# Joint blocks all begun early, and early gate blocks of the last feed-forward as fills of the second sequence

## The chip, the cores and the metric

The kernel runs on one core of a Trainium2 chip. The time is that of the device, in microseconds, from one launch of the whole program; the runs given are separate executions of the same program. One further execution was recorded by the hardware profiler, and all rows below come from it. Engines are named as in the profile: PE (TensorE) multiplies and transposes into PSUM, DVE (VectorE), ACT (ScalarE) and POOL (GpSimd) work elementwise, SP issues most of the DMAs. The engines run on their own, each through its instructions in a fixed order, and wait for one another by semaphores.

## The reference

One layer of an encoder, in float32, over two sequences of 512 tokens ("prompt" and "sample") of width 1024:

- a SwiGLU feed-forward, `x + 0.5 * (silu(n @ w_gate) * (n @ w_up)) @ w_down` with `n = rms_norm(x)` and 2816 hidden columns;
- a mixing block on `h = rms_norm(x)` and `proj = h @ w_in`: grouped-query attention (8 query heads of 64, 2 key heads, RMS norm of queries and keys, rotary angles, softmax over all 512 tokens), and beside it a bidirectional mLSTM with 4 heads of 128, whose gates are 16 columns of the projection; both are projected up, gated by `sigmoid` of further columns, added, and go through `w_out` onto `x`;
- a second SwiGLU feed-forward, and a final RMS norm.

Both sequences use the same weights and do not depend on each other.

## The kernel before

Every product is done in three matmuls on values split into a high part and a remainder (`split`, `put`, `w_pair`: a copy on ACT that rounds, and a subtraction on another engine), each 128 x 128 by 512 columns.

**Seven products for eight.** In the feed-forwards and in the "joint" projections, the two sequences (and two halves of the inner dimension, and two weight columns) form a 2 x 2 block product, done in seven products (Strassen's scheme in Winograd's form): `B11, B21, B22, T1..T4`. The right sides `xc[...]` are made from both sequences by `right_sums` (line 281). Of a block's seven products, two (`B11`, `B21`) need the first sequence only. So a block can be *begun* (`Up.begin`, line 441, and `Joint.begin`, line 755): 24 matmuls into PSUM, evicted through a ring `k` of two tiles and stored to DRAM (`kept`). The *rest* (`gu_rest`, line 350, and `Joint.block`) has five products, 60 matmuls; a block that was not begun has all 84. While the second sequence's sides are still being made, 10 blocks of each feed-forward (of 22) and 10 of the joint (of 14) are begun; `ORDER` and `JORDER` then alternate begun and whole blocks. The left sides are made per block from the raw weights by `gu_left_a`, `gu_left_b` and `gu_left_c`, and the results of a pair of blocks are turned into the right sides of the down product by `Sides`.

**Program order and queues.** The program is written as a sequence of Python calls; a tile framework then orders each engine's instructions by priority (the place in the program, shifted by `shifted(n)`) and by when operands are there, and adds the waits. So what stands early in the program tends to run early, and work that is listed together is interleaved.

**The stages.** First feed-forward (to about 650 us): begin, rest, `ffn_down`. Joint (to about 940): 14 blocks that give both sequences' merge gates, output gates, and mLSTM queries and keys, parked in `jbuf`; blocks 10 to 13, queries and keys, are stored split. Then `mix(s, ...)` for `s = 0` and `s = 1`, a generator that the program advances with `next`: per-token projections (`tok_proj`), *rotations* (gates, key and query norm and rotary, with transposes on PE), attention (`scores`, `attend`, eight heads), memory heads (`mem_head`, `mem_out`, four), merge (`merge_mem`, eight units), output product (`out_unit`, eight units of 24 matmuls). A list `queue` holds units with which PE is filled between heads: `fill(fills[h])` after each of the eight attention heads and four memory heads takes as many units as the table `FILLS` says, `fill(99)` takes the rest. The first sequence's fills are projections of the second one's queries and values (eight units of 48 narrower matmuls), the second one's are six of the first sequence's output units. `prep2` normalises the first sequence's rows for the last feed-forward. Last come that feed-forward and its down product with the final norm.

The order of the second half of the mix, before:

```
    next(m1)                  # second sequence: rotations
    next(m0)                  # first: merge
    outs0, acc0_ = next(m0)
    go(*outs0[:OUT])          # OUT = 2 output units
    queue.extend(outs0[OUT:])
    next(m1)                  # second: attention, memory heads, with fills
```

## Time and profile before

| | |
|---|---|
| median of 3 runs | 2169.08 us (2168.52 to 2169.25) |
| the profiled execution | 2165.41 us |
| its span, first to last instruction | 2163.6 us |
| mean granted clock of PE over the span | 0.978 |
| PE busy | 2070.3 us, 96% |
| DVE busy | 1677.2 us, 78% |
| ACT busy | 944.9 us, 44% |
| POOL busy | 93.1 us, 4% |

A row of stages gives, for a stretch of the span, each engine's busy time and its number of instructions, the clock that the throttle granted to PE as a share of full speed, and the share of the DMA engines. A row of groups gives line, engine, operation, output and inputs, shape and count, then busy time and mean duration in nanoseconds, then the engine's idle time just before them and what ended it. A row of the timeline gives start and duration in us. Rows of the DMA view end with the median us from issue to landing. POOL's spans are rough, and the line numbers are those of the kernel before.

### The profile page before, as it was taken

Reading aid. Unit: us, or ns where it says so; the run is one execution under the profiler, and the core shown is the slowest. Engines: PE = TensorE matmul, PEld = TensorE weight load, DVE = VectorE, ACT = ScalarE, POOL = GpSimd, SP = SyncE. Lnnn points to the kernel's source line nnn. Section 1 sums busy time; section 2 is a strip of 40 time slices with the busy share of each in tenths; the row PEclk is TensorE's granted clock in tenths of the full one; section 3 lists DMA queues with packets and bytes.
Section 4 is the critical chain, followed back from the end, with each engine's and each line's share of the span. In section 5 each row is a group of like instructions: output and inputs, shape, how many; then the busy total and the mean of one; then the engine's idle time right before and its main releaser. Section 6 shows DMA issues by size and latency. Waiting matters only on the chain.

```text
span 2163.6 us, 27752 instructions
## 1 busy us (share of the span) xinstructions
PE 2070.3 (96%) x9502; PEld 1691.9 (78%) x9502; DVE 1677.2 (78%) x3043; ACT 944.9 (44%) x1744; POOL 93.1 (4%) x106
## 2 busy tenths in 40 slices
PE   8999999999998999999998596899999999999998
PEld 6888888888877788888786474678888888888887
DVE  7888887877898877655878787674888888786697
ACT  6544444432234433354666355442544444443222
POOL 0000000000012000000001110102000000000000
PEclk9999999999999999999999698999999999999999
DMA  8655654798757555586256341578855565499753
GB/s 275 192 193 172 219 185 146 256 360 316 251 190 226 162 170 173 145 296 227 88 186 218 108 165 59 195 251 297 267 161 178 193 198 170 159 338 352 270 211 113
DMA packets 332557, 450.70 MB, mean 208 GB/s; under 512 B 21488, under 2 KB 198720, under 8 KB 331392
## 3 DMA queue, kind: packets, MB, share of 16 engines
q1 hardware_dynamic: 330544, 443.46, 60.9%
q0 software_dynamic: 1872, 5.46, 0.8%
q8 instruction: 75, 1.23, 0.2%
q14 instruction: 66, 0.54, 0.1%
HBM read 288.25 MB, written 160.60 MB: 207 GB/s over the span
## 4 chain that ended last, share of the span: by engine, by line
PE 84%; DVE 8%; DMA 3%; ACT 3%; issue 1%; POOL 0%; SPq 0%; DVEq 0%; ACTq 0%; POOLq 0%
PE pss L333 22%; PE pst L333 14%; PE mm L333 11%; PE mm L589 8%; PE mm L915 5%; PE pst L589 4%; PE pss L589 4%; PE pso L589 2%; PE mm L867 2%; PE mm L898 2%; PE pss L1206 1%; PE pst L1225 1%; PE pso L1233 1%; PE pso L1356 1%; PE pss L915 1%
## 5 line engine op out<-in xcount | busy, mean ns | idle before, releaser
L333 PE MATMUL mm<-xc,w 128*128 128x512 f32 x1392 | 334.8, 392 | 6.9 <-DVE f L752 2.5
L333 PE MATMUL pss<-xc,w 128*128 128x512 f32 x1392 | 337.3, 391 | 0.2 <-DVE t L364 0.2
L333 PE MATMUL pst<-xc,w 128*128 128x512 f32 x1392 | 334.7, 389 | 0.0
L333 PEld LDWEIGHTS mm<-xc,w 128*128 128x128 f32 x1392 | 261.0, 189 | 65.4 <-DVE w L292 4.3
L333 PEld LDWEIGHTS pss<-xc,w 128*128 128x128 f32 x1392 | 259.8, 188 | 60.8 <-DVE t L364 6.8
L333 PEld LDWEIGHTS pst<-xc,w 128*128 128x128 f32 x1392 | 261.3, 188 | 54.3
L291 ACT ACTIVATE w<-t 128x512 fp32r<-128x512 f32 x232 | 140.8, 627 | 183.4 <-issue 55.2
L292 DVE TENSOR_TENSOR w<-t,w 128x512 fp32r<-128x512 f32 x232 | 155.8, 690 | 69.1 <-ACT w L291 66.6
L589 PE MATMUL mm<-rt,w 128*128 128x512 f32 (+1 forms) x819 | 188.6, 384 | 0.0
L589 PEld LDWEIGHTS mm<-rt,w 128*128 128x128 f32 x819 | 151.2, 188 | 29.8
L333 PE MATMUL pss<-xc,f 128*128 128x512 f32 x696 | 167.3, 389 | 0.1
L333 PEld LDWEIGHTS pss<-xc,f 128*128 128x128 f32 x696 | 130.6, 188 | 27.6 <-DVE t L797 0.5
L657 ACT ACTIVATE w<-wr 128x512 fp32r<-128x512 f32 x72 | 45.1, 632 | 138.2 <-PE pso L589 71.1
L657 ACT ACTIVATE w<-t 128x512 fp32r<-128x512 f32 x82 | 51.8, 632 | 108.1 <-PE pst L589 63.1
L292 DVE TENSOR_TENSOR w<-wr,w 128x1024 fp32r<-128x1024 f32 x58 | 72.7, 1257 | 28.4 <-ACT w L291 28.4
L589 PE MATMUL pss<-rt,w 128*128 128x512 f32 x396 | 93.8, 389 | 0.4 <-issue 0.4
L589 PE MATMUL pst<-rt,w 128*128 128x512 f32 x396 | 93.6, 389 | 0.0
L915 PE MATMUL mm<-mh,w 128*128 128x512 f32 x256 | 85.2, 406 | 1.9 <-ACT w L239 1.3
L589 PEld LDWEIGHTS pss<-rt,w 128*128 128x128 f32 x396 | 74.2, 188 | 16.2 <-ACT w L657 0.8
L589 PEld LDWEIGHTS pst<-rt,w 128*128 128x128 f32 x396 | 74.3, 188 | 15.4
L291 ACT ACTIVATE w<-wr 128x1024 fp32r<-128x1024 f32 x58 | 61.2, 1056 | 52.2 <-PE pst L333 21.6
L658 DVE TENSOR_TENSOR t<-pst,t 128x512 fp32r<-128x512 f32 x96 | 64.8, 688 | 22.6 <-ACT t L657 19.2
(356 smaller groups left out, 3537.2 us busy)
## 6 DMA issues: line engine op xcount, KB each, us to landing
rt<-rbuf SPq DMA_DIRECT2D x154, 512.0 KB, 5.5
wr<-in_ffn_w_gate_dram SPq DMA_DIRECT2D x62, 512.0 KB, 5.4
rbuf<-tab SPq DMA_DIRECT2D x102, 256.0 KB, 4.0
wpark<-w SPq DMA_DIRECT2D x48, 512.0 KB, 3.6
wr<-in_w_in_dram SPq DMA_DIRECT2D x45, 512.0 KB, 4.4
wr<-in_ffn_w_up_dram SPq DMA_DIRECT2D x44, 512.0 KB, 4.6
rbuf<-f SPq DMA_DIRECT2D x72, 256.0 KB, 3.8
rbuf<-R SPq DMA_DIRECT2D x68, 256.0 KB, 4.0
```

The source lines that it names most:

```text
L291: pin(nc.scalar.activation(t[:, 0], src, AF.Copy))
L292: pin(V_.tensor_tensor(t[:, 1], src, f(t[:, 0]), op=ALU.subtract))
L333: nc.tensor.matmul(p, a[:, k, :], xt[:, b, k, :], start=(first and k == 0 and i == 0), stop=(k == HK_ - 1 and i == 2), skip_group_check=True)
L589: nc.tensor.matmul(p, u[:, a, d * P:(d + 1) * P], r[:, b, ts], start=(first and q == 0 and k == 0), stop=(q == len(us) - 1 and k == 2), sk ...
L657: nc.scalar.activation(hi, src, AF.Copy)
L658: (eng or V_).tensor_tensor(lo, src, f(hi), op=ALU.subtract)
L867: nc.tensor.matmul(p[b][:, :N], a[:, bs], w_[:, kl, :], start=(k == 0 and i == 0), stop=(k == KD - 1 and i == 2))
L898: nc.tensor.matmul(p[b // 2][:, (b % 2) * HW:(b % 2 + 1) * HW], a[:, bs], w_[:, kl, :], start=(k == 0 and i == 0 and b % 2 == 0), stop=(k ...
L915: nc.tensor.matmul(p, a[:, k, :], b, start=(k == 0 and i == 0), stop=(k == n - 1 and i == 2))
L1206: nc.tensor.matmul(p, qT[:, h, b * P:(b + 1) * P], kv[:, hk * 2 + j, :], start=(j == 0), stop=(j == 1))
L1225: nc.tensor.transpose(p[:, b * P:(b + 1) * P], Ps[b][:, kb * P:(kb + 1) * P], ident)
L1233: nc.tensor.matmul(po, Vst[:, kv_, hk, :], w, start=(kv_ == 0 and i == 0), stop=(kv_ == 3 and i == 1))
```

## The change

- **Joint:** all 14 blocks are begun (`JORDER` has no whole block left); begun blocks 10 to 13 take the tile for their high part from the ring `k`. In the joint's preparation the remainders of `B22` and `T3` are made on POOL.
- **Mix, first sequence:** the rotations stand in the program ahead of the value projection and of the second sequence's key projection. The second sequence's values are parked in DRAM (`vpark`) by `rows_ahead` and split in its memory heads by `parked_values`.
- **Mix, order:** the first sequence's merge comes before the second's rotations; then all eight output units are issued, then statistics and `prep2`, all ahead of the second's attention.
- **Fills of the second sequence:** eight gate blocks of the last feed-forward are begun there (`Up.early`, `EARLY = 8`), each with a weight split, 24 matmuls, a copy and a Silu on ACT, and two stores. The last feed-forward begins ten more in its own preparation, so 18 of its 22 blocks are begun; its order (`order_of`) spreads the four whole ones among 16 begun. The first feed-forward keeps its order.
- **Engines:** the softmax scaling (`tensor_scalar` in `scores`) goes from DVE to POOL in both sequences; the mask add of `mem_rows` goes to POOL in the second too; query and key tiles of the second come from the buffers `w8` instead of `wr`; the last of each sequence's sums of squares (`sq_add` in `done1`) goes from POOL to DVE.

```diff
@@ -278,14 +278,14 @@
...
-    def right_sums(xc, k, x0l, x0u, x1l, x1u):
+    def right_sums(xc, k, x0l, x0u, x1l, x1u, eng=None):
...
         for i, t in ((T1, x0l), (T2_, x1u), (T3, x1l), (T4, x0u)):
-            put(xc[i], k, t)
+            put(xc[i], k, t, eng if i == T3 else None)
@@ -417,19 +417,33 @@
...
     LATER, SOONER = 100,-100
-    AHEAD = 10
+    AHEAD, EARLY = 10, 8
...
     LAST = 2
-    ORDER = [j for p in zip(range(AHEAD - LAST), range(AHEAD, NF)) for j in p]
-    ORDER += list(range(2 * AHEAD - LAST, NF)) + list(range(AHEAD - LAST, AHEAD))
+    def order_of(ahead):
+        begun, whole = list(range(ahead - LAST)), list(range(ahead, NF))
+        out = []
+        while begun or whole:
+            if begun and (not whole or len(begun) * (NF - ahead) >= len(whole) * (ahead - LAST)):
+                out.append(begun.pop(0))
+            else:
+                out.append(whole.pop(0))
+        return out + list(range(ahead - LAST, ahead))
+    ORDERS = [[j for p in zip(range(AHEAD - LAST), range(AHEAD, NF)) for j in p], order_of(AHEAD + EARLY)]
+    ORDERS[0] += list(range(2 * AHEAD - LAST, NF)) + list(range(AHEAD - LAST, AHEAD))
...
-        def __init__(self, xc, wg, wu, rb):
-            self.xc, self.rb = xc, rb
+        def __init__(self, xc, wg, wu, rb, order):
+            self.xc, self.rb, self.order = xc, rb, order
             self.v = [w.rearrange("(k p) c -> p k c", p=P) for w in (wg, wu)]
             self.kept, self.open = {}, None
+        def make_rings(self):
             self.ring = Rings(s=["t2"] * 3, wd=["f2"] * 2, v=["t2"] * 3, h=["t2"] * 5, o=["f2"] * 2 + ["R"] * 2)
@@ -458,8 +472,19 @@
...
+        def early(self, j):
+            def comp(W):
+                self.kept[j] = kept[j]
+                t, u = T2(F32, "f2"), T2(F32, "f2")
+                X = gu_first_a(W, self.xc, t)
+                nc.sync.dma_start(kept[j][0], t)
+                gu_first_b(X, W, self.xc, u)
+                nc.sync.dma_start(kept[j][1], u)
+            return (lambda: self.left(j)), comp
         def rest(self, raw, at=None, hook=None):
-            ring = self.ring
+            ring, ORDER = self.ring, self.order
@@ -502,7 +527,7 @@
...
-    def ffn_down(wd, rb, ring, tail, xres, done, at_step, hook, halves=None):
+    def ffn_down(wd, rb, order_, ring, tail, xres, done, at_step, hook, halves=None):
         n = n_steps
@@ -526,7 +551,7 @@
...
             t = free.pop(0)
-            fb = ORDER[2 * fp + i]
+            fb = order_[2 * fp + i]
             for c in range(2):
@@ -708,9 +733,8 @@
...
     JP += [(768 + h * P, 1280 + h * P) for h in range(4)]
-    NJ, RAW, JAHEAD, JLAST = 14, 10, 10, 4
-    JORDER = [j for p in zip(range(JAHEAD - JLAST), range(JAHEAD, NJ)) for j in p]
-    JORDER += [j for j in range(NJ) if j not in JORDER]
+    NJ, RAW = 14, 10
+    JORDER = [0, 1, 10, 2, 3, 11, 4, 5, 12, 6, 7, 13, 8, 9]
     jbuf = [[[dpool.tile([P, 2, S] if j >= RAW else [P, S], F32, name=f"jbuf{s}_{j}_{u}") for u in range(2)]
@@ -728,10 +752,10 @@
...
-        def out(self, s, j, u, t):
+        def out(self, s, j, u, t, kind="h"):
             to = jbuf[s][j][u]
             if j >= RAW:
-                hi = self.ring("h")
+                hi = self.ring(kind)
                 split(t, hi.bitcast(F32R), t.bitcast(F32R))
@@ -746,11 +770,11 @@
...
-        def first_b(self, X, W, j, t):
+        def first_b(self, X, W, j, t, kind="h"):
             product(X, W[B21], self.xc[B21], False)
...
                 V_.tensor_tensor(t, X, R[0], op=ALU.mult)
-            self.out(0, j, 0, t)
+            self.out(0, j, 0, t, kind)
@@ -764,7 +788,7 @@
...
                 j, X, W = self.open
-                self.first_b(X, W, j, self.ring("k"))
+                self.first_b(X, W, j, self.ring("k"), "k")
             self.open = None
@@ -954,28 +978,29 @@
...
-    def tok_queries_ahead(s, src, half):
+    vpark = dpool.tile([P, 4, S], F32, name="vpark")
+    def rows_ahead(park, s, src, col, half):
         def done(p):
...
                     nc.scalar.activation(t[:, u * HW:(u + 1) * HW], p[b], AF.Copy, scale=r[s][:, b:b + 1])
-                nc.sync.dma_start(qpark[:, 2 * i:2 * i + 2, half * HW:(half + 1) * HW],
+                nc.sync.dma_start(park[:, 2 * i:2 * i + 2, half * HW:(half + 1) * HW],
                                   t.rearrange("p (u c) -> p u c", u=2))
-        return tok_half(src, 0, half, done)
-    def tok_values_ahead(s, src, half):
-        def done(p):
-            if half == 0:
-                value_tile(s)
-            for b in range(4):
-                values_done(s, p[b], b, slice(half * HW, (half + 1) * HW))
-        return tok_half(src, 1792, half, done)
-    FILLS = ((0, 1, 1, 1, 1, 1, 0, 1, 2, 0, 0, 0), (0, 1, 0, 1, 0, 1, 0, 0, 1, 1, 1, 0))
-    def mix(s, src=None, after=None, fills=None):
+        return tok_half(src, col, half, done)
+    def parked_values(s):
+        vm = value_tile(s)
+        for b in range(4):
+            t = T2()
+            nc.sync.dma_start(t, vpark[:, b])
+            split(t, vm[:, 0, b, :], vm[:, 1, b, :])
+    FILLS = ((0, 1, 1, 1, 1, 1, 1, 0, 0, 0, 0, 0), (0, 0, 1, 1, 1, 1, 1, 0, 1, 1, 0, 0))
+    def mix(s, src, fills):
@@ -1126,14 +1151,10 @@
...
         def load_qk(h):
-            if s == 0:
-                t = wpool.tile([P, 4, S], F32R, tag="w8", bufs=4, name=nm("qk"))
-                halves = t[:, 0:2], t[:, 2:4]
-            else:
-                halves = [wpool.tile([P, 2, S], F32R, tag="wr", bufs=4, name=nm("qk")) for _ in range(2)]
-            for u, t in enumerate(halves):
-                nc.sync.dma_start(f(t), jbuf[s][RAW + h][u])
-            qks[h] = [t[:, i] for t in halves for i in range(2)]
+            t = wpool.tile([P, 4, S], F32R, tag="w8", bufs=4, name=nm("qk"))
+            for u in range(2):
+                nc.sync.dma_start(f(t[:, 2 * u:2 * u + 2]), jbuf[s][RAW + h][u])
+            qks[h] = [t[:, i] for i in range(4)]
@@ -1156,8 +1177,7 @@
...
             go(*tok_proj(src, QC, 2, q_done))
-            go(*tok_values(0, src))
-            yield None
+            flush()
         else:
@@ -1174,7 +1194,7 @@
...
             em3 = em.rearrange("p (b s) -> p b s", b=4)
-            (G_, V_)[s].tensor_tensor(em3, eb3, tabs[3][:, d].unsqueeze(1).to_broadcast([P, 4, P]), op=ALU.add)
+            G_.tensor_tensor(em3, eb3, tabs[3][:, d].unsqueeze(1).to_broadcast([P, 4, P]), op=ALU.add)
             return eb3, em3
@@ -1210,7 +1230,7 @@
...
                 V_.reciprocal(c[:, 2:3], c[:, 1:2])
-                V_.tensor_scalar(e, e, c[:, 2:3], None, op0=ALU.mult)
+                G_.tensor_scalar(e, e, c[:, 2:3], None, op0=ALU.mult)
                 Ps.append(e)
@@ -1287,8 +1307,6 @@
...
                 split(mg[:, d, :], mh[:, d, :], ml[:, d, :], G_ if d < 6 and s == 0 else V_)
-                if after:
-                    after(d)
             return up_unit(1, d, mem, done, (PS, PT)[d % 2])
@@ -1366,6 +1384,8 @@
...
         ups = [merge_att(d) for d in range(KD)]
+        if s:
+            parked_values(s)
         load_qk(0)
@@ -1411,10 +1431,12 @@
...
     xc = [None] * 7
-    up = Up(xc, I["ffn1_w_gate"][0], I["ffn1_w_up"][0], rbuf[0])
+    up = Up(xc, I["ffn1_w_gate"][0], I["ffn1_w_up"][0], rbuf[0], ORDERS[0])
+    up.make_rings()
     xins = [I[n][0] for n in ("x_prompt", "x_sample")]
...
-    kept = [[dpool.tile([P, S], F32, name=f"kept{j}_{i}") for i in range(2)] for j in range(AHEAD)]
+    kept = [[dpool.tile([P, S], F32, name=f"kept{j}_{i}") for i in range(2)]
+            for j in range(AHEAD + EARLY)]
@@ -1509,7 +1531,7 @@
...
         nc.sync.dma_start(xbuf[s][:, d, :], xs[s][:, d, :])
-        accs[s] = sq_add(xs[s][:, d, :], accs[s], "R")
+        accs[s] = sq_add(xs[s][:, d, :], accs[s], "R", eng=V_ if d == (KD - 1, DH - 1)[s] else None)
         if s == 0 and d == KD - 1:
@@ -1529,7 +1551,7 @@
...
-    ffn_down(I["ffn1_w_down"][0], rbuf[0], up.ring, tail, xbuf, done1, 7, mix_consts)
+    ffn_down(I["ffn1_w_down"][0], rbuf[0], up.order, up.ring, tail, xbuf, done1, 7, mix_consts)
@@ -1547,27 +1569,27 @@
...
             normed(t, gm, R[s_], kk)
-        for j in ((3,), (4, 5), (6, 7), (8, 9))[k]:
+        for j in ((3, 4), (5, 6, 7), (8, 9, 10), (11, 12, 13))[k]:
             jt.begin(j, jt.left(j))
-        put(xc[B22], k, x1u)
-        right_sums(xc, k, x0l, x0u, x1l, x1u)
+        put(xc[B22], k, x1u, G_)
+        right_sums(xc, k, x0l, x0u, x1l, x1u, G_)
     jt.begun()
...
     src1 = lambda k: (nhl[1][0][:, k, :], nhl[1][1][:, k, :])
-    m0 = mix(0, src0, None, FILLS[0])
+    m0 = mix(0, src0, FILLS[0])
     next(m0)
+    go(*tok_values(0, src0))
     for d in range(KD):
...
     flush()
-    next(m0)
     for hf in range(2):
-        queue.extend(tok_queries_ahead(1, src1, hf))
+        queue.extend(rows_ahead(qpark, 1, src1, 0, hf))
     for hf in range(2):
-        queue.extend(tok_values_ahead(1, src1, hf))
+        queue.extend(rows_ahead(vpark, 1, src1, 1792, hf))
     next(m0)
@@ -1587,15 +1609,19 @@
...
     OUT = 2
-    m1 = mix(1, None, prep2, FILLS[1])
+    m1 = mix(1, None, FILLS[1])
+    next(m0)
     next(m1)
-    next(m0)
     outs0, acc0_ = next(m0)
-    go(*outs0[:OUT])
-    queue.extend(outs0[OUT:])
-    next(m1)
+    go(*outs0)
+    flush()
     acc2[0] = acc0_[0]
     stats2(0)
+    for d in range(KD):
+        prep2(d)
+    up = Up(xc, I["ffn2_w_gate"][0], I["ffn2_w_up"][0], rbuf[1], ORDERS[1])
+    queue.extend(up.early(j) for j in range(EARLY))
+    next(m1)
     next(m1)
@@ -1603,14 +1629,15 @@
...
-    up = Up(xc, I["ffn2_w_gate"][0], I["ffn2_w_up"][0], rbuf[1])
+    up.make_rings()
     raw0 = up.fetch(0)
-    W = [gu_left_a(raw0[0])]
-    up.begin(0, W[0])
+    j0 = EARLY
+    W = [up.left(j0)]
+    up.begin(j0, W[0])
     stats2(1)
-    W += [up.left(j) for j in (1, 2)]
-    up.begin(1, W[1])
-    up.begin(2, W[2])
+    W += [up.left(j0 + j) for j in (1, 2)]
+    up.begin(j0 + 1, W[1])
+    up.begin(j0 + 2, W[2])
     for i in (T2_, T1, T3, B22, T4):
@@ -1621,7 +1648,7 @@
...
         for j in ((3,), (4, 5), (6, 7), (8, 9))[k]:
-            up.begin(j, up.left(j))
+            up.begin(j0 + j, up.left(j0 + j))
         put(xc[B22], k, x1u)
@@ -1706,7 +1733,7 @@
...
-    ffn_down(I["ffn2_w_down"][0], rbuf[1], up.ring, tail, x2buf, done2, n_steps - 7, load_fn, halves=True)
+    ffn_down(I["ffn2_w_down"][0], rbuf[1], up.order, up.ring, tail, x2buf, done2, n_steps - 7, load_fn, halves=True)
...
 def host_consts():

```

## The prediction

> **What bounds the kernel now.** I read the page first, for the shares and the chain, then the time by stages, then the groups of the stages that lose time. The page:
>
> ```profile
> span 2163.6 us, 27752 instructions
> ...
> PE 2070.3 (96%) x9502; PEld 1691.9 (78%) x9502; DVE 1677.2 (78%) x3043; ACT 944.9 (44%) x1744; POOL 93.1 (4%) x106
> ...
> PE 84%; DVE 8%; DMA 3%; ACT 3%; issue 1%; POOL 0%; SPq 0%; DVEq 0%; ACTq 0%; POOLq 0%
> ```
>
> TensorE (PE) bounds the kernel: 96% busy and 84% of the chain. The order of the built instructions shows that the change keeps every product and transpose, so only time that PE now loses can be won. Where it is lost, by stages (columns: width, then busy time and count of each engine, granted clock, DMA share, GB/s):
>
> ```profile
> core 0: us, PE busy (x) PEld busy (x) DVE busy (x) ACT busy (x) POOL busy (x), PEclk, DMA share, GB/s
> 640.00:740.00 100.00, 90.61 (x391) 71.96 (x391) 87.42 (x147) 44.18 (x66) 15.24 (x10) 0.98 0.62 193
> 1010.00:1110.00 100.00, 92.56 (x594) 78.57 (x594) 83.40 (x197) 69.48 (x163) 4.26 (x12) 0.98 0.37 118
> 1110.00:1190.00 80.00, 73.34 (x386) 59.23 (x384) 63.26 (x181) 48.42 (x115) 10.33 (x6) 0.96 0.65 219
> 1190.00:1254.00 64.00, 42.05 (x172) 33.60 (x171) 51.80 (x129) 24.28 (x43) 11.33 (x6) 0.71 0.40 135
> 1254.00:1335.00 81.00, 68.23 (x316) 48.84 (x314) 62.54 (x131) 43.59 (x99) 6.12 (x7) 0.95 0.24 86
> 1335.00:1450.00 115.00, 98.19 (x424) 72.58 (x425) 77.00 (x232) 57.75 (x142) 6.10 (x7) 0.90 0.68 224
> 1450.00:1510.00 60.00, 59.38 (x257) 48.32 (x257) 34.15 (x57) 17.40 (x26) 11.23 (x12) 0.98 0.73 263
> 1545.00:1805.00 260.00, 260.00 (x1141) 213.44 (x1140) 216.56 (x336) 116.20 (x194) 0.00 (x0) 1.00 0.58 186
> ```
>
> A stage's loss is its width less PE's busy time times the granted clock: the joint's preparation 100 - 90.61 x 0.98 = 11.2 us; rotations and attention of the first sequence 9.3; its memory heads 9.6; the bubble around the second's rotations 34.1; attention of the second 16.2; its memory heads 26.6; its merge and output product 1.8; the last feed-forward 0. Together 109 us. The bubble seen from PE:
>
> ```profile
> 1207.09 2.86 PE L1068 MATMUL pst<-ident,qT 128*128 128x128 f32 x12
> 1219.22 1.94 PE L1152 MATMUL pst<-ident,t 128*128 128x128 f32 x8 [9.28 <-DVE t L658]
> ```
>
> PE holds nothing but rotation transposes there and waits 9.28 us for VectorE (DVE).
>
> **The change part by part.** A product of twelve full-width matmuls sets PE's pace:
>
> ```profile
> 743.03 2.72 PE pss L333 x12
> ```
>
> An output unit, or an early gate block, is 24 such matmuls: 5.44 us.
>
> **(a) Rotations of the second sequence behind the first's merge, with all eight output units beside them: -26.** In the new order PE's 32 rotation transposes are scattered through 192 output matmuls, 8 x 5.44 = 43.5 us of PE. The first two output units stood right behind the bubble, the other six were fills of the second's heads. The bubble's own PE work is 42.05 x 0.71 = 30 us, so the stretch holds 73 us less the two units that it partly had. DVE's 51.80 us, plus 8 residual adds of 0.7 and 8 wide weight splits,
>
> ```profile
> L292 DVE TENSOR_TENSOR w<-t,w 128x512 fp32r<-128x512 f32 x232 | 155.8, 690 | 69.1 <-ACT w L291 66.6
> ...
> L292 DVE TENSOR_TENSOR w<-wr,w 128x1024 fp32r<-128x1024 f32 x58 | 72.7, 1257 | 28.4 <-ACT w L291 28.4
> ```
>
> of 1.26, some of which the stretch has already, is some 65 us: below PE. The loads of the output weights, `x2buf` stores (POOL's queue) and parked query rows go through queues that are at a DMA share of 0.40 here. I take 8 us lost in place of 34: the last memory head's chain (4) and the ends (4). Bounds: 3 (PE full) to 20 (only half covered).
>
> **(b) First sequence: -6.** Its rotations now lie beside the value and key projections, and the softmax scaling (L1213) goes from DVE to GpSimd (POOL). DVE and ScalarE (ACT) work of a head, from the attention of the second:
>
> ```profile
> L1209 DVE TENSOR_REDUCE asm<-pss 128x1 f32<-128x512 f32 x32 | 21.6, 684 | 1.2 <-PE pss L1206 1.2
> L658 DVE TENSOR_TENSOR t<-pst,t 128x512 fp32r<-128x512 f32 x24 | 16.4, 688 | 5.2 <-ACT t L657 4.3 <-PE pst L1225 0.7
> L1213 DVE TENSOR_SCALAR t<-t,asm 128x512 f32<-128x512 f32 x30 | 15.6, 524 | 0.6
> L1212 DVE RECIPROCAL asm<-asm 128x1 f32<-128x1 f32 x30 | 4.7, 158 | 4.7 <-ACT t L1211 4.4
> ```
> ```profile
> L1211 ACT ACTIVATE t<-pss,asm 128x512 f32<-128x512 f32 x31 | 21.1, 684 | 11.2 <-DVE asm L1209 8.1 <-DVE asm L1212 3.0
> L657 ACT ACTIVATE t<-pst 128x512 fp32r<-128x512 f32 x24 | 13.6, 597 | 14.2 <-PE pso L1233 12.1 <-PE pst L1225 2.0
> L1211 ACT ACTIVATION_READ_ACCUMULATOR t<-pss,asm 128x1 f32 x30 | 5.9, 196 | 0.0
> ```
>
> Each head has four of each: DVE 4 x (0.684 + 0.688 + 0.524 + 0.158) = 8.2, and about 1 for joining the output, 9.2 us; without the scaling 7.1. PE has 16 matmuls and 16 transposes, about 5.4 us, and a fill's 5.4. So a filled head goes from a tie of DVE and PE to PE's 10.8. Six of eight heads keep a fill: 9.3 lost becomes 3. Bounds 1 to 9. POOL must do the scaling of a head within that time. No trace shows it at this width; the nearest rows are
>
> ```profile
> L679 POOL TENSOR_SCALAR hn<-hn 128x4 f32<-128x4 f32 x1 | 0.2, 225 | 6.0 <-DMA hn<-in_mlstm_head_norm_dram 6.0
> L692 POOL TENSOR_SCALAR gb<-gb 128x64 f32<-128x64 f32 x1 | 0.4, 373 | 6.8 <-DMA gb<-in_q_norm_dram 6.8
> L156 POOL TENSOR_TENSOR R<-R,f 128x512 f32<-128x512 f32 x17 | 25.1, 1479 | 148.3 <-ACT f L155 140.3 <-ACT R L152 7.5
> ```
>
> The slope of the first two, 148 ns over 60 elements, gives 0.37 + 448 x 0.0025 = 1.5 us, as much as the two-input add of full width; ends 0.4 and twice 1.5. Four are 6 us a head, one head ahead of their use: hidden, and if not, rival two.
>
> **(c) First sequence's memory heads: 0.** The last two value units move from the first head to the end, where the last head's chain needs cover; the heads get thinner. Value units lose their DVE split (it is made from a parked copy in the second sequence, four splits of 0.69, four stores and four loads).
>
> **(d) Attention of the second: +2.** Gone from it: six output units and the merge's normalisation. Added: eight early gate blocks, the normalisation of the first sequence's rows (16 DVE operations) and the statistics ahead of it. At the start PE has only 18 score matmuls (4 us) and the first transposes (2) until four normalised rows are there. In DVE's built order 21 full-width operations (0.63 us by part h) and 19 small ones (0.158 as L1212) stand between the last output unit and the fourth row, 13 + 3 us, and the handovers to PE and ACT add 2: 18 us, 12 of them lost and new. Later ACT binds. Its head is 4 x (0.684 + 0.196 + 0.597) and about 0.9 for joining, 6.8 us; an early block adds a weight copy, two evictions and, since Silu and Exp alternate, table loads. The built order has 12 more of these than before:
>
> ```profile
> L291 ACT ACTIVATE w<-wr 128x1024 fp32r<-128x1024 f32 x58 | 61.2, 1056 | 52.2 <-PE pst L333 21.6
> ```
> ```profile
> L348 ACT ACT_TABLE_LOAD x1 | 1.3, 1283 | 2.5 <-issue 2.5
> ```
>
> A block costs ACT 1.06 + 2 x 0.6 + 2 x 1.28 = 4.8 us, a filled head 11.6 against PE's 10.8. Five filled heads lose 1 us each, the start 12, the thin last head 1: 18 against 16.2. Bounds 10 and 38 (every load on the chain, 15.4, and the start doubled). The Trainium skill, "ScalarE: Activation LUTs", in the rules for kernel authors, budgets about 2.7 us for every switch to another set, and says to do all of one set before switching; the same page has 1283 ns for the load itself, as the row here. By the budget an estimate of 12 x 2.7 = 32 us would stand in place of 15.4 and the time would be 17 us longer if all of it bound. I go by the row.
>
> **(e) Memory heads of the second: -14.** Here the chain had loads in it:
>
> ```profile
> by line: PE mm L915 32.9%; PE pso L1356 10.2%; DMA wr<-in_w_out_dram 9.5%; DMA box<-ebuf 8.5%; PE pst L1348 7.2%; ACT t L1320 6.0%; PE pss L1306 3.4%; PE pss L915 2.0%; issue 1.9%; ACT w L239 1.9%; PE pst L1225 1.7%; PE pst L203 1.5%; ACT t
> ```
>
> Of 115 us, 9.5% (11 us) is waiting for output weights, whose buffers (`wr`) the query and key tiles held, and 8.5% (10 us) for gate rows. The change moves query and key tiles to `w8` and the mask add to POOL, as the first sequence has them, which loses 9.6 us in the same stage. Three early blocks fill it as three output units did. 26.6 becomes 12.5: the first sequence's 9.6 and two pairs of table loads. Bounds 8 and 24. The stores of early blocks stand in SP's queue waiting for a Silu; the next head's loads queue behind, which is in the upper bound.
>
> **(f) Merge of the second: +1**, the thin last head; the normalisation leaves this stage.
>
> **(g) Joint: 0.** Four more begun blocks cover 4 x 5.44 us of DVE-bound preparation (DVE 87.42 of 100), which would win up to 6. Against it: each of the four stores three tiles through the two-tile ring `k`:
>
> ```profile
> kept<-f SPq DMA_DIRECT2D x50, 256.0 KB, 3.3
> jbuf<-f SPq DMA_DIRECT2D x10, 256.0 KB, 2.2
> ```
>
> An eviction (0.7), a landing (3.3), a copy and a subtraction (1.3) and another landing (2.2) make 7.5 us a block against 5.44: four times 2.1, 8 us, of which three PSUM tiles hide about half. DVE queues behind these evictions. The eight splits given to POOL take 0.69 us each from DVE, but:
>
> ```profile
> 653.19 2.07 DVE L292 TENSOR_TENSOR w<-wr,w 128x1024 fp32r<-128x1024 f32 x1
> ```
> ```profile
> 652.89 12.08 POOL L156 TENSOR_TENSOR R<-R,f 128x512 f32<-128x512 f32 x7 [7.54 <-ACT R L152]
> ```
>
> beside seven POOL adds of 1.73 us a DVE split took 2.07, some 0.8 longer than its wide form elsewhere: 8 x 0.8 = 6.4 against 5.5 won. Bounds of the term -6 and +8. The Trainium skill, "SBUF — State Buffer", section on who interferes with whom, calls the shared port an exclusive lock between a DVE instruction with two SBUF inputs and a GpSimd one that reads SBUF. By it the eight would block DVE for their whole 8 x 1.5 us, an estimate of +6 for the term instead of 0; the trace's stretch is milder.
>
> **(h) Last feed-forward: +3.** 18 of 22 blocks are begun, in runs of four. A begun block has 60 matmuls left, 13.6 us; by `gu_left_b`, `gu_left_c`, `gu_rest` and `Sides` it has 21.5 DVE operations of 512 columns (8, 1, 7 and half of 11), at the stage's (216.56 - 10 x 1.2) / 326 = 0.63 us 13.5 us. Before, a whole block (84 matmuls, 19 us) stood between any two. Ends: 0 (PE is full already, so no gain), and at 0.69 us a piece 18 x 1.2 = 22. I take it near the lower, since DVE's row sits at 216.56 of 260 with PE never idle. Each block more begun also stores and loads 1 MB and fetches its gate weights twice, hidden at a DMA share of 0.58.
>
> Sum: -26 - 6 + 2 - 14 + 1 + 3 = -40. The profiled execution took 2165.41 us (span 2163.6); the median of the three runs is 2169.08, 3.7 above it. So 2125 against the profile, 2129 as a median.
>
> **The rivals.** One: smaller gain. ACT switching and the late first fill bind (d), and transposes still hold up output units in (a), 20 us together: 2149. For it: both are new waits on in-order engines. Against: the output units need nothing of the rotations.
>
> Two, slower: POOL's scaling. It sets the pace of a head when four of them exceed 11 us. Over 16 heads the 40 us are used up at 16 x (4T - 11) = 40, T = 3.4 us; at T = 4 the time is 2129 + 80 = 2209. Against it: no full-width POOL group here is over 2 us. For it: the operation is in no trace.
>
> Three, larger gain: (a) 3, (b) 1, (d) 10, (e) 8, (g) -6, (h) 0 gives 2129 - 5 - 2 - 8 - 5 - 6 - 3 = 2100.
>
> Four: no change, (a) and (e) given back in (d) and (h), whose upper bounds add 20 + 19 = 39 to the forecast: 2168.
>
> **How the numbers follow.** Forecast 2109 to 2140: 0.56. Rival three 0.15, one 0.17, four 0.03, two 0.09. The range 2095 to 2160 leaves out two, four and some of three. A measurement here tells 0.2% (4.3 us) from no change: faster 0.88, same 0.03, slower 0.09.
>
> **What would show it.** After the change the stretch of output units should show PE at over 0.9 with rotations inside, and granted clock near 1.0; the second's memory heads no DMA in the chain; POOL scalings near 1.5 us; table loads 19 in all; the last feed-forward PE still full. The forecast is wrong if POOL scalings end PE's waits, if DVE rows of the last feed-forward release PE, or if the first early product is over 15 us late.

## The result, and the profile after

| | before | after |
|---|---|---|
| median, us | 2168.8 (2162.3 to 2169.3) | 2110.8 (2105.1 to 2111.6) |
| profiled execution, us | 2165.41, span 2163.6 | 2110.19, span 2108.3 |
| PE busy, us (same 9502 matmuls) | 2070.3 | 2044.0 |
| mean granted clock | 0.978 | 0.994 |

The ratio of the times is 0.9734, with a 95% interval of 0.9709 to 0.9759: 58 us won where 40 were forecast. The page of the changed kernel:

```profile
PE 2044.0 (97%) x9502; PEld 1678.3 (80%) x9502; DVE 1650.0 (78%) x2961; ACT 960.4 (46%) x1760; POOL 212.9 (10%) x184
...
L1233 POOL TENSOR_SCALAR t<-t,asm 128x512 f32<-128x512 f32 x64 | 100.8, 1589 | 54.5 <-DVE asm L1232 41.0
```

The span is 55.3 us shorter. PE's busy time fell by 26.3 us with the same matmuls, which is the clock, and its idle time from 93.3 to 64.3, which is 29.0. So nearly half of the gain is matmuls that run faster because PE pauses less before them. The softmax scaling on GpSimd took 1589 ns, where 1.5 us were estimated.

To see where the time went I cut both executions at the same events: first product of the joint; first token product; first product of the first sequence's memory heads; the last product of those heads; first score of the second sequence; first product of its memory heads; the last one of those; 66 us later; last product of the last feed-forward; end (the rows of the end are not shown). Time by stages before (columns as in the prediction: width, busy time of PE, PE's loads, DVE, ACT and POOL, granted clock, DMA share, GB/s):

```profile
659.60:938.70 279.10, 271.28 (x1185) 221.88 (x1184) 206.46 (x322) 109.89 (x176) 5.21 (x3) 0.99 0.59 182
938.70:1094.70 156.00, 148.41 (x904) 127.89 (x904) 106.37 (x248) 89.89 (x193) 3.03 (x20) 0.99 0.57 193
1094.70:1189.50 94.80, 88.14 (x482) 72.35 (x481) 74.65 (x207) 60.78 (x147) 12.90 (x8) 0.96 0.64 210
1189.50:1254.80 65.30, 43.35 (x176) 34.27 (x175) 52.02 (x129) 24.34 (x43) 11.33 (x6) 0.71 0.41 140
1254.80:1335.80 81.00, 67.43 (x313) 48.36 (x312) 62.81 (x131) 44.38 (x101) 6.12 (x7) 0.94 0.23 83
1335.80:1441.20 105.40, 91.43 (x392) 67.67 (x393) 70.37 (x207) 55.72 (x138) 6.10 (x7) 0.90 0.66 216
1441.20:1507.20 66.00, 63.34 (x277) 50.94 (x277) 39.08 (x78) 17.04 (x26) 10.67 (x11) 0.97 0.77 278
1507.20:1935.90 428.70, 428.53 (x1885) 351.98 (x1884) 355.57 (x557) 193.52 (x320) 2.84 (x3) 1.00 0.62 204
```

The same view after:

```profile
659.10:944.00 284.90, 274.02 (x1185) 224.30 (x1184) 208.24 (x315) 109.66 (x176) 15.27 (x10) 0.98 0.63 191
944.00:1100.20 156.20, 151.88 (x929) 131.09 (x927) 97.10 (x223) 93.00 (x199) 54.45 (x54) 0.99 0.61 205
1100.20:1176.50 76.30, 74.00 (x428) 62.44 (x427) 64.59 (x191) 54.54 (x135) 9.59 (x7) 1.00 0.62 209
1176.50:1258.10 81.60, 76.99 (x375) 62.55 (x374) 68.72 (x144) 37.50 (x62) 23.36 (x19) 1.00 0.92 308
1258.10:1336.80 78.70, 67.58 (x316) 48.43 (x314) 62.34 (x129) 55.90 (x115) 48.93 (x32) 0.96 0.40 131
1336.80:1433.00 96.20, 87.22 (x423) 67.93 (x422) 68.12 (x196) 71.06 (x156) 14.14 (x10) 1.00 0.62 200
1433.00:1499.00 66.00, 65.12 (x290) 53.27 (x289) 28.37 (x50) 15.38 (x22) 12.96 (x13) 1.00 0.76 251
1499.00:1880.40 381.40, 379.81 (x1672) 312.37 (x1671) 343.05 (x548) 174.75 (x293) 0.61 (x2) 1.00 0.73 239
```

The loss of a stage is again its width less PE's busy time times the clock. Row by row:

| stage (step) | loss before | loss after | measured | forecast |
|---|---|---|---|---|
| joint (g) | 10.5 | 16.4 | +5.9 | 0 |
| attention of the first (b) | 9.1 | 5.8 | -3.3 | -6 |
| memory heads of the first (c) | 10.2 | 2.3 | -7.9 | 0 |
| bubble, or merge and outputs (a) | 34.5 | 4.6 | -29.9 | -26 |
| attention of the second (d) | 17.6 | 13.8 | -3.8 | +2 |
| memory heads of the second (e) | 23.1 | 9.0 | -14.1 | -14 |
| its merge and outputs (f) | 4.6 | 0.9 | -3.7 | +1 |
| last feed-forward (h) | 0.2 | 1.6 | +1.4 | +3 |
| end | 11.5 | 11.6 | +0.1 | |

The measured terms add up to the span's 55.3 us. The clock is given to 0.01, which is 0.8 us in an 80 us stage and 1.6 in one of 156, and the first attention of the same code lost between 3.7 and 7.6 us in nine executions of this study; differences under 3 us in one stage are not told apart. The bubble is gone. What waited for DVE before the rotations, 9.28 us at one place, is now this (PE's two largest groups of waits in the stretch of merge and outputs: in all, times, longest):

```profile
PE pst L1173 <- DVE t L683: 2.3, 2, 1.5
PE pst L1136 <- DVE et L1134: 1.9, 1, 1.9
```

The start of the second's attention, up to the first early product; then PE's largest group of waits in that whole stage; then, in its memory heads, PE's largest group of waits and its only one for a load:

```profile
1258.10:1274.60 16.50, 10.38 (x38) 6.65 (x36) 13.67 (x37) 8.76 (x21) 13.74 (x9) 0.79 0.45 129
```
```profile
PE pss L1226 <- ACT t L1231: 8.1, 9, 1.9
```
```profile
PE pst L1366 <- DVE t L1352: 2.2, 2, 1.4
PE mm L939 <- DMA w<-wpark: 1.6, 2, 0.8
```

L1231 is ACT's Exp; where it waits itself, it waits for DVE's maximum or reciprocal (7.3 us in that stage). None of PE's waits in the memory heads ends with a load of raw weights or gate rows.

### The profile page after: what moved, and what is told of

Same layout as the page of the kernel before. It is cut to its first block, busy times and chain, and to the rows that moved or that the text cites. A ratio compares the mean times of both kernels' runs of the same rounds, so it can differ in the third digit from the quotient of the medians.

```text
span 2108.3 us, 28067 instructions
## 1 busy us (share of the span) xinstructions
PE 2044.0 (97%) x9502; PEld 1678.3 (80%) x9502; DVE 1650.0 (78%) x2961; ACT 960.4 (46%) x1760; POOL 212.9 (10%) x184
## 5 line engine op out<-in xcount | busy, mean ns | idle before, releaser
L333 PE MATMUL mm<-xc,w 128*128 128x512 f32 x1392 | 339.1, 396 | 14.0 <-DVE w L292 4.0
L292 DVE TENSOR_TENSOR w<-t,w 128x512 fp32r<-128x512 f32 x232 | 155.8, 689 | 69.0 <-ACT w L291 66.3
L1233 POOL TENSOR_SCALAR t<-t,asm 128x512 f32<-128x512 f32 x64 | 100.8, 1589 | 54.5 <-DVE asm L1232 41.0
L292 DVE TENSOR_TENSOR w<-wr,w 128x1024 fp32r<-128x1024 f32 x58 | 74.9, 1296 | 17.9 <-ACT w L291 17.9
L614 PEld LDWEIGHTS pst<-rt,w 128*128 128x128 f32 x396 | 74.4, 188 | 15.4
```

Source lines behind the costliest of these rows:

```text
L292: pin(V_.tensor_tensor(t[:, 1], src, f(t[:, 0]), op=ALU.subtract))
L333: nc.tensor.matmul(p, a[:, k, :], xt[:, b, k, :], start=(first and k == 0 and i == 0), stop=(k == HK_ - 1 and i == 2), skip_group_check=True)
L614: nc.tensor.matmul(p, u[:, a, d * P:(d + 1) * P], r[:, b, ts], start=(first and q == 0 and k == 0), stop=(q == len(us) - 1 and k == 2), sk ...
L1233: G_.tensor_scalar(e, e, c[:, 2:3], None, op0=ALU.mult)
```

## The experiments

Each kernel is the changed one with the edit shown, unless it says otherwise. Times were taken beside runs of the kernel before, which had medians of 2165 to 2166 us there; by its ratio of 0.9734 the changed kernel stands at about 2108 beside these. So the ratio is what to compare, also where an expectation names a time beside 2111: a difference of 0.0010 in the ratio is 2.2 us.

| experiment | median, us | ratio to before (95%) |
|---|---|---|
| the change | 2110.8 | 0.9734 (0.9709 to 0.9759) |
| 1 rotations ahead of the merge | 2134.2 | 0.9858 (0.9837 to 0.9879) |
| 2 value units sooner | 2126.8 | 0.9823 (0.9802 to 0.9845) |
| 3 query and key tiles in `wr` | 2124.8 | 0.9816 (0.9794 to 0.9838) |
| 4 early blocks behind the heads | 2128.6 | 0.9834 (0.9811 to 0.9857) |
| 5 joint as before | 2107.7 | 0.9733 (0.9719 to 0.9748) |
| 6 joint's splits on DVE | 2100.0 | 0.9702 (0.9687 to 0.9716) |
| 7 scaling on DVE | 2116.7 | 0.9777 (0.9762 to 0.9791) |
| 8 early gates without Silu | 2101.6 | 0.9697 (0.9681 to 0.9713) |
| 9 as 6, Silu put off | 2095.5 | 0.9681 (0.9668 to 0.9694) |
| 10 half of the splits on DVE | 2108.0 | 0.9735 (0.9722 to 0.9749) |
| 11 first rotations late | 2111.6 | 0.9751 (0.9738 to 0.9764) |
| 12 as 9, first scaling on DVE | 2097.1 | 0.9683 (0.9670 to 0.9696) |

### 1. Is it the order, or the output units (step a)?

```
-    next(m0)
     next(m1)
+    next(m0)
     outs0, acc0_ = next(m0)
```

> The changed kernel with one line swapped: the rotations of the second sequence are issued before the first's merge, as before the change; all eight output units still follow together, and everything else stays. Loss of a stage is its width less PE's busy time times its granted clock; in the changed kernel merge, rotations and output units of the first sequence (1179 to 1262 us) lose 6.0 us, where the kernel before lost 34.1. Theory, the order decides: PE's queue holds transposes whose rows DVE has not made, and nothing behind them can pass, so the stretch loses 25 to 34 us again and the time is 2130 to 2140. Rival, the output units decide: as the scheduler may put merge and output products between the transposes anyway, the stretch loses under 12 us and the time stays within 6 us of 2111.

The stretch from the last memory head to the first score, and the rotations in it as PE saw them:

```profile
1175.50:1282.00 106.50, 84.12 (x375) 68.65 (x374) 66.70 (x144) 38.00 (x62) 25.71 (x19) 0.84 0.73 240
```
```profile
1207.89 1.94 PE L1173 MATMUL pst<-ident,t 128*128 128x128 f32 x8 [10.13 <-DVE t L683]
1211.38 1.94 PE L1173 MATMUL pst<-ident,t 128*128 128x128 f32 x8 [1.54 <-DVE t L683]
```

Two more like the second follow. The bubble is back, almost to the digit (9.28 and three times 1.54 before), though all the merge's last products and the eight output units stood right behind it. The stretch loses 35.8 us, 22.4 of them idle time and 13.5 a clock of 0.84. The order decides; PE did not pass a transpose whose rows were not ready.

### 2. What the value units cover (step c)

```
-    FILLS = ((0, 1, 1, 1, 1, 1, 1, 0, 0, 0, 0, 0), (0, 0, 1, 1, 1, 1, 1, 0, 1, 1, 0, 0))
+    FILLS = ((0, 1, 1, 1, 1, 1, 0, 1, 2, 0, 0, 0), (0, 0, 1, 1, 1, 1, 1, 0, 1, 1, 0, 0))
```

> The changed kernel with the old list of fills for the first sequence: the last two value units stand in the last attention head and the first memory head instead of behind the last memory head. The prediction gave this step (c) 0. The trace has the first memory heads at a loss of 2.3 us against 9.6 before. Theory, the value units cover the chain of the last memory head: the loss returns to 8 to 10 us, the time is 2117 to 2119, and PE waits for DVE at the end of the heads. Rival, the gain came from elsewhere (thinner DVE work of value units, or loads): the loss stays under 4 us and the time at 2111 within 3.

Memory heads of the first, then merge and outputs, then attention of the second:

```profile
1102.00:1188.10 86.10, 79.96 (x442) 64.87 (x441) 64.07 (x187) 53.41 (x130) 8.43 (x6) 0.98 0.69 227
1188.10:1274.20 86.10, 76.50 (x344) 60.66 (x343) 64.96 (x143) 35.29 (x57) 19.90 (x16) 0.94 0.73 243
1274.20:1354.90 80.70, 69.59 (x315) 49.61 (x314) 62.36 (x130) 56.30 (x116) 52.37 (x36) 0.92 0.40 134
```

The losses are 7.7, 14.2 and 16.7 against 2.3, 4.6 and 13.8. By the ratio the time is 19 us longer. The theory had the mechanism and less than half of its size: the last head's chain runs on into the merge. (The 2.9 in the second's attention are within what a stage varies by.) PE's two largest waits between 1170 and 1285 us, the first in the second's attention and the other in the merge:

```profile
PE pss L1226 <- ACT t L1231: 3.8, 3, 1.6
PE pst L213 <- DVE rs L192: 3.3, 1, 3.3
```

L213 turns the last head's sums. So of the 29.9 us under (a), about 10 are due to the two value units.

### 3. The buffers of query and key tiles (step e)

```
-            t = wpool.tile([P, 4, S], F32R, tag="w8", bufs=4, name=nm("qk"))
+            if s == 0:
+                t = wpool.tile([P, 4, S], F32R, tag="w8", bufs=4, name=nm("qk"))
...
+            else:
+                halves = [wpool.tile([P, 2, S], F32R, tag="wr", bufs=4, name=nm("qk")) for _ in range(2)]
```

> The changed kernel with the query and key tiles of the second's memory heads in the buffers wr again, as before. Step (e) took 14 us from the end of two waits for loads, one of them 11 us for weights whose buffers these tiles held. Theory, the buffers: the raw weights of early blocks, which go through wr as output weights did, wait for a head to free its tiles; memory heads of the second lose 9.0 us now and would lose 15 to 20, time 2117 to 2122. Rival, the waits were the queue's and not the buffers': loss within 3 us of 9.0 and time within 3 of 2111.

Memory heads of the second:

```profile
1336.60:1447.40 110.80, 94.27 (x417) 70.56 (x416) 68.83 (x196) 71.84 (x156) 13.98 (x10) 0.92 0.56 182
```

They lose 24.1 us in place of 9.0, as much as before the change (23.1). That is above the expected 15 to 20. Giving back the buffers alone undoes step (e), with the mask add still on GpSimd. The theory's path is shown in part only: 3.5 us of ACT's waits in these heads now end with a load of raw gate weights, which none did in the changed kernel, but PE's longest wait, 5.3 us, ends with DVE.

### 4. Are the early blocks worth more between the heads than behind them?

```
-    FILLS = ((0, 1, 1, 1, 1, 1, 1, 0, 0, 0, 0, 0), (0, 0, 1, 1, 1, 1, 1, 0, 1, 1, 0, 0))
+    FILLS = ((0, 1, 1, 1, 1, 1, 1, 0, 0, 0, 0, 0), (0,) * 12)
```

> The changed kernel without fills in the second sequence: the eight early blocks all run behind the last memory head, the same work in another place. Theory, the prediction's sums: attention of the second is then paced by ACT (8 heads of 6.8 us and a start of some 10, 64 us in place of 75) and its PE work there shrinks by 5 blocks or 27 us, so 16 us are lost; the memory heads lose three blocks' cover, some 10 us; together 2137, between 2125 and 2150. Rival one, the fills are worth nothing because PE could run the blocks later as well: 2111 within 4. Rival two, without cover each head shows its whole chain of handovers: 8 heads of 12 us and more, 2155 or above.

Attention and memory heads of the second:

```profile
1257.20:1331.70 74.50, 53.92 (x238) 36.03 (x236) 59.70 (x126) 45.33 (x103) 46.28 (x31) 0.91 0.40 128
1331.70:1423.10 91.40, 78.22 (x371) 59.22 (x372) 70.52 (x200) 61.98 (x146) 14.60 (x11) 0.96 0.41 129
```

The two lose 25.4 and 16.3 us against 13.8 and 9.0. That is 19 us, and by the ratio the time is 22 us longer, where the theory had 26 with bounds of 14 and 39. The attention took 74.5 us and not the 64 that ACT's work alone would give, and ACT was busy for 45.3 of them: a head without a fill seems to be held by its handovers, not by ACT's work.

### 5, 6 and 10. What the joint's two edits cost (step g)

5 undoes both; 6 leaves all blocks begun early and takes GpSimd's splits back; 10 takes half of them back.

```
(6)  -        put(xc[B22], k, x1u, G_)
     -        right_sums(xc, k, x0l, x0u, x1l, x1u, G_)
     +        put(xc[B22], k, x1u)
     +        right_sums(xc, k, x0l, x0u, x1l, x1u)
(10) -        put(xc[B22], k, x1u, G_)
     +        put(xc[B22], k, x1u)
(5)  as 6, and
     -    JORDER = [0, 1, 10, 2, 3, 11, 4, 5, 12, 6, 7, 13, 8, 9]
     +    JORDER = [j for p in zip(range(JAHEAD - JLAST), range(JAHEAD, NJ)) for j in p]
     ...
     -        for j in ((3, 4), (5, 6, 7), (8, 9, 10), (11, 12, 13))[k]:
     +        for j in ((3,), (4, 5), (6, 7), (8, 9))[k]:
```

> The changed kernel with the joint blocks as they were before the change: ten begun early, the old order, all splits on DVE. The prediction gave the change of this step (g) 0, with bounds of 6 won and 8 lost. In the traces the first token product comes at 944.0 us in the changed kernel and at 938.7 before. Theory, beginning all blocks early costs 5 us: the first token product comes at 938 to 940 and the time is 2105 to 2107, the best of all so far. Rival, the later time is drift between executions (it was 942.1 to 944.9 in other runs with the same joint): the product comes at 942 or later and the time is 2111 within 2.

> The changed kernel with only the eight splits of the joint's preparation back on DVE; all blocks are still begun early. It parts the two costs of step (g). Theory one, GpSimd and DVE slow each other (the forecast had 6.4 us lost against 5.5 won): the first token product comes 1 to 5 us earlier than 944. Theory two, the store ring of two tiles is what costs (up to 8 us): DVE, with 5.5 us more work, is later still, and the product comes at 944 to 948.

> The changed kernel with four of the eight splits of the joint's preparation on GpSimd (those of one term), the other four on DVE. From the joint's first product to the first token product it takes 275.1 us with none on GpSimd and 280.6 to 285.3 with eight. Theory, each such split blocks DVE operations with two SBUF inputs until it ends, and its own 1.3 to 2.0 us lie in a chain: the cost goes with their number, 278 to 281 us and a time of 2103 to 2107. Rival, it is the order that the scheduler chose for eight: 275 to 277 or 283 and more.

The joint from its first product to the first token product, in 5, 6 and 10:

```profile
659.40:941.20 281.80, 272.37 (x1186) 223.49 (x1186) 206.77 (x323) 110.04 (x176) 3.14 (x2) 0.99 0.56 179
```
```profile
658.40:933.50 275.10, 269.67 (x1185) 220.89 (x1184) 206.23 (x323) 109.43 (x176) 3.12 (x2) 1.00 0.64 198
```
```profile
659.20:938.60 279.40, 271.24 (x1186) 222.51 (x1185) 206.68 (x319) 109.18 (x176) 9.08 (x6) 0.99 0.63 195
```

With all blocks begun early it takes 275.1 us with no split on GpSimd (274.7 and 276.9 in experiments 9 and 12), 279.4 with four, and 280.6 to 285.3, with a mean of 283.3, in eight executions with eight. So the eight splits cost some 7.7 us. A part of it stands in DVE's busy time: the changed kernel took eight splits of 0.68 us off DVE (323 operations to 315), and DVE was busy for 208.24 us in place of 206.23. In the changed kernel, GpSimd's first three splits and DVE's operations at them:

```profile
680.51 1.29 POOL L279 TENSOR_TENSOR xc<-t,xc 128x512 fp32r<-128x512 f32 x1 [18.20 <-DMA wr<-in_w_in_dram]
684.81 1.75 POOL L279 TENSOR_TENSOR xc<-t,xc 128x512 fp32r<-128x512 f32 x1 [3.01 <-DVE f L776]
688.52 1.58 POOL L279 TENSOR_TENSOR xc<-t,xc 128x512 fp32r<-128x512 f32 x1 [1.96 <-ACT xc L278]
```
```profile
680.28 0.69 DVE L770 TENSOR_TENSOR f<-mm,R 128x512 f32<-128x512 f32 x1
680.88 1.47 DVE L284 TENSOR_TENSOR t<-t,t 128x512 f32<-128x512 f32 x1
685.34 1.78 DVE L279 TENSOR_TENSOR xc<-t,xc 128x512 fp32r<-128x512 f32 x1
688.90 3.42 DVE L292 TENSOR_TENSOR w<-wr,w 128x1024 fp32r<-128x1024 f32 x2
```

GpSimd's first split ends at 680.51 + 1.29 = 681.80; the DVE subtraction that began within it ends at 682.35, 0.55 us later, and the next pair (686.56 and 687.12) has the same distance. So it was at all four splits of experiment 10 and at six of the eight here; at a seventh, the third, the DVE operation (the first of the two at 688.90) was of double width and ended at 691.18, 1.08 us behind. Together these seven DVE operations took 5.9 us longer than the same operations elsewhere in the stage. DVE's product that reads PSUM (L770) and overlaps the split keeps its 0.69. In one case (713.68) it was GpSimd that took longer, 2.02 us, beside a DVE operation begun earlier.

With 5.9 us longer against 5.5 us taken off, DVE's busy time alone does not make 7.7. What does is seen at PE. Its waits for DVE's wide splits (L292) and its products from PSUM (L770) between 655 and 765 us, in the changed kernel and then in 6:

```profile
PE mm L333 <- DVE f L770: 3.8, 1, 3.8
PE mm L333 <- DVE w L292: 3.2, 1, 3.2
```
```profile
PE mm L333 <- DVE w L292: 1.0, 1, 1.0
PE mm L333 <- DVE f L770: 0.8, 2, 0.6
```

The wait of 3.2 us ends at 691.24, right behind the wide split that GpSimd's third one held up (691.18). The one of 3.8 us ends at 744.03, behind the last split on GpSimd; what brings it about was not followed further. All eight executions with eight splits have both, of 2.4 to 3.4 and of 2.4 to 4.1 us; with four only the second is there (4.6 us), and with none neither is over 1.8. Between these two executions PE's idle time is 10.9 us of the stage against 5.4, and the rest of the difference is the clock, 0.98 against 1.00. So the cost is no steady 1 us a split: most of it is two pauses of PE and the lower clock behind them.

The joint as before took 281.8 us in experiment 5 and 279.1 in the kernel before, against means of 275.6 with no split on GpSimd and 283.3 with eight, and the ratio of 5 is that of the changed kernel. The expected 938 to 940 for the first token product was missed at 941.2: the two edits of the joint are a gain of some 5 us and a loss of some 8 that nearly cancel. Experiment 10's theory holds for the joint, 279.4, but not for the time, whose ratio of 0.9735 is that of the change: its memory heads, with no edit in them, lost 4.1 and 11.0 us in place of 2.3 and 9.0.

### 7. Softmax scaling on DVE (steps b and d)

```
-                G_.tensor_scalar(e, e, c[:, 2:3], None, op0=ALU.mult)
+                V_.tensor_scalar(e, e, c[:, 2:3], None, op0=ALU.mult)
```

> The changed kernel with the softmax scaling of both sequences on DVE again, 64 operations, of 1589 ns each on GpSimd and of 524 ns on DVE before. Theory, steps (b) and (d): DVE has 2.1 us more in each head and ties with PE in the filled ones; the first attention (5.8 us lost) loses 8 to 10, the second (13.8 lost) 15 to 18, the time is 2115 to 2119. Rival, the longer operation on GpSimd stretches each head's chain by a microsecond, and DVE had room: the two stages lose less than now and the time is 2105 to 2109.

Attention of the first, and of the second:

```profile
939.20:1088.60 149.40, 145.45 (x905) 126.76 (x904) 105.52 (x247) 89.56 (x192) 2.88 (x20) 1.00 0.60 205
...
1252.90:1341.00 88.10, 74.64 (x317) 53.45 (x316) 73.95 (x161) 56.68 (x116) 3.63 (x4) 0.88 0.36 123
```

They lose 4.0 and 22.4 us against 5.8 and 13.8. By the ratio the time is 9 us longer, a little above the theory's 4 to 8, and nearly all of it arises in the second sequence: eleven executions with its scaling on GpSimd and its fills in place lost 12.7 to 17.7 in the same stage. There DVE also normalises and splits the feed-forward's rows, and it goes from 62.3 us busy to 74.0.

### 8. Table loads (step d)

```
-                gu_first_b(X, W, self.xc, u)
+                gu_first_b(X, W, self.xc, u, AF.Copy)
```

with `gu_first_b` evicting by the function that it is given.

> The changed kernel with a plain copy in place of Silu when an early gate block is evicted, so the gates of eight blocks lack their Silu; every other operation stays. Silu and Exp alternate in the changed kernel between the second's heads; without it the table loads of 1283 ns there go (12 more than before the change). Theory of step (d), ACT binds the filled heads by 1 us each and a third of the loads lies on the path: attention and memory heads of the second, which lose 13.8 and 9.0 us, lose 5 to 8 less together, time 2103 to 2106. Rival one, the budget of about 2.7 us a switch binds each time: 25 us or more less, below 2090. Rival two, the loads fall where ACT waits: no change, 2111 within 3.

Attention and memory heads of the second:

```profile
1256.60:1336.20 79.60, 69.02 (x322) 49.18 (x321) 64.48 (x134) 53.76 (x118) 51.25 (x33) 0.96 0.40 133
1336.20:1423.90 87.70, 83.27 (x404) 64.72 (x403) 65.28 (x192) 58.27 (x142) 10.48 (x8) 1.00 0.65 212
```

They lose 13.3 and 4.4 us: 0.5 less and 4.6 less. By the ratio the whole kernel gains 8 us; the rest lies in stages without an edit. The sum of 5 is the theory's, its place is not. Part of the reason is where the loads fall: of the 12 that the change added, only four came before the memory heads, from 1315.9 us on, as two early blocks were done by then. PE's waits for ACT's Exp in the attention stay at 8.0 us, against 8.1, so these loads did not make them.

### 9. A version that beats both

```
+                self.raw.add(j)
-                gu_first_b(X, W, self.xc, u)
+                gu_first_b(X, W, self.xc, u, AF.Copy)
...
+                if j in self.raw:
+                    nc.scalar.activation(got[1], got[1], AF.Silu)
```

on top of 6.

> The changed kernel with two things put together: all eight splits of the joint's preparation on DVE (that version took 2100.0 us), and the Silu of the eight early gate blocks put off, so that they are evicted and parked by a plain copy between the heads, and a Silu of 512 columns is applied when the last feed-forward loads them back. The result is the reference's. Theory: the memory heads of the second lose 4.4 us as with the plain copy, in place of 9.0, and eight Silus of 0.6 us on ACT lie beside PE in the last feed-forward, where ACT is busy for under half: 2094 to 2097. Rival: the Silu stands between a load and its use, and PE waits for it in the last feed-forward: the feed-forward loses 4 us or more there and the time is 2099 or above.

Memory heads of the second, and the last feed-forward:

```profile
1328.60:1415.80 87.20, 83.33 (x405) 64.68 (x404) 65.47 (x192) 58.09 (x142) 10.96 (x8) 1.00 0.65 213
1481.80:1868.60 386.80, 383.43 (x1683) 313.80 (x1683) 343.85 (x549) 180.81 (x303) 2.73 (x3) 1.00 0.71 236
```

The heads lose 3.9 us; the feed-forward loses 3.4 where it lost 1.6, so a little of the rival is true. At 0.9681 of the time before, this is 11 us faster than the change. Against 6 it is 4.5 us, and the two intervals overlap.

### 11. The place of the first sequence's rotations (step b)

```
             go(*tok_proj(src, QC, 2, q_done))
-            flush()
+            go(*tok_values(0, src))
+            yield None
...
     next(m0)
-    go(*tok_values(0, src0))
     for d in range(KD):
         prep1(d)
     go(*tok_keys_ahead(1, src1))
     flush()
+    next(m0)
```

> The changed kernel with the rotations of the first sequence put back behind its value projection and the second's key projection, as before the change; the softmax scaling stays on GpSimd. It parts step (b), which had 6 us for both together. From the first token product to the first memory head's product the changed kernel loses 5.8 us, the kernel before 9.1. Theory, the place of the rotations is the gain: PE meets the transposes with nothing behind them, the stretch loses 9 to 11 again, time 2114 to 2117. Rival, the gain was the scaling on GpSimd: the stretch loses 6 within 1, time 2108 to 2112. (With the scaling on DVE and the rotations early it lost 4.0, which speaks for the theory.)

The stretch lost 6.9 us, within what the same code shows and as the rival has it. By the ratio of 0.9751 the time is 3.7 us above the change's, at the theory's lower end, but the two intervals overlap. Neither this nor experiment 7 brings the old 9.1 back; which part of (b) made its 3 us stays open.

### 12. Scaling of the first sequence on DVE

The edit of 7 for `s == 0` alone, on top of 9.

> The best version so far (splits of the joint on DVE, late Silu, 2095.5 us) with the softmax scaling of the first sequence back on DVE and that of the second on GpSimd. With both on DVE the first attention lost 4.0 in place of 5.8, the stretch of the output units 7.5 in place of 4.6, the second attention 22.4 in place of 13.8. Theory: the first sequence has DVE time to spare, so GpSimd's 1589 ns buys nothing there: 2095 within 3, and the second attention's loss stays at 13 to 15. Rival, GpSimd's longer operation costs the first sequence its chain: 2090 to 2092. Rival two, the first sequence needs it as the second does: 2100 or above.

The time is that of 9 (0.9683 and 0.9681), as the theory has it. The second attention, whose code is that of 9, lost 17.7 us outside the expected 13 to 15, at a granted clock of 0.90; so this stage varies by some 4 us between executions of the same code.

## Why the prediction was right, and where its terms were wrong

The side, the range and the largest terms held; the profile gained 55.3 us where the sum had 40. The interval that had most weight, 2109 to 2140, held by less than 2 us, and that is luck: the time lies nearer to rival three's 2100 than to the forecast 2129. The misses partly cancel: (c), (d), (a), and (e) with (f) gave 22 us more than forecast, (g) and (b) 9 us less. By the steps:

- **(a) -26, measured -29.9: right in its mechanism.** PE filled the stretch to 77.0 of 81.6 us at full clock, and experiment 1 shows that it is the order. Its reading was too narrow in one thing: some 10 us of it are the value units' (2). Without their cover 14.2 us stay lost, within its bounds of 3 and 20 but not its 8.
- **(b) -6, measured -3.3.** The step "without the scaling" gave the first sequence what it does not need; experiments 7 and 12 show nothing won there by GpSimd.
- **(c) 0, measured -7.9: the step that failed most.** It noted that the last head's chain "needs cover" and priced the cover at nothing. Experiment 2 puts it at some 15 to 18 us over two or three stages (5.4, 9.6 and 2.9).
- **(d) +2, measured -3.8.** The start, from the first score to the first early product, took 16.5 us where 18 were forecast, and lost 16.5 - 10.38 x 0.79 = 8.3 of them where 12 were. "Later ACT binds" was not borne out: the 12 loads were there as counted (19 in all against 7), but only four of them came in this stage, and taking them out moved it by 0.5 us. PE's waits end with ACT's Exp (8.1 us), and the Exp's own with DVE (7.3 us); with DVE's scaling back the stage lost 22.4. So the scaling's move, which the sum credited to the first sequence, is worth some 5 to 10 us in the second. (The upper bound of 38 is 39 by its own parts, 15.4 and twice 12.)
- **(e) -14, measured -14.1, and (f) +1, measured -3.7.** Of loads, PE now waits for parked weights (`wpark`) alone in these heads, 1.6 us. The price of table switching is here (4.6 us), with eight of the 12 loads. (f) is mostly the other cut of the stages: before, the tail of the heads fell into it. So the two have to be taken together, -17.8 against -13, and the agreement of (e) to 0.1 is luck of the cut.
- **(g) 0; +5.9 between the two profiles, +3 between means.** The sum's balance was near; both of its parts were too small. More begun blocks won some 5 us between means (the forecast had up to 6, less what its ring of two would take), and the eight splits cost 7.7, where the forecast had 6.4 against 5.5. "Some 0.8 longer", read from one DVE split beside seven GpSimd adds, held in sum: 5.9 us at seven operations. The failed step is that only DVE's busy time was counted: PE's two pauses, 3.2 and 3.8 us, and the lower clock behind them had no price. The Trainium skill, "SBUF — State Buffer", section "Who interferes with whom", says that one of the two blocks fully for the whole instruction, and that DVE reading at most one input from SBUF, outside its two-port modes, does not contend. The trace agrees with it on both points, by the 0.55 us behind the end and by the 0.69 of the product from PSUM. By it the prediction had +6 for this term, an estimate from 12 us of blocking; 5.9 were seen, so that it came near 7.7 is luck.
- **(h) +3, measured +1.4: right.** DVE is at 343.05 of 381.4 us and ends PE's waits only now and then (its largest group: twice, 1.4 us in all).

For table switches the Trainium skill, "ScalarE: Activation LUTs", in the rules for kernel authors, budgets about 2.7 us each; 12 of them would be 32 us. Taking them out gained 5 us in the two stages that hold them, 0.4 each, and 8 by the ratio of the whole, so the sum was right to stay with the row of 1283 ns; its bound of 15.4 was not reached either.

Of the rivals, two (GpSimd's scaling) fell with 1589 ns against a threshold of 3.4 us. One needed (a) and (d), four (d) and (h), to be worse than forecast, and all three came out better. Three came nearest: its (a) of 3, (e) of 8 and (h) of 0 were almost met (4.6, 9.0 and 1.6), its (b) of 1 and (d) of 10 were not (5.8 and 13.8), and its (g) of -6 came only in experiment 6.
